# Expert-choice routing on 32 partitions with a threshold, modulation sums of 512 columns, and a final norm by token block

## The chip, the cores and the metric

The kernel runs on one core of one Trainium2 chip. The core has five engines that run side by side and wait for each other by semaphores: TensorE (PE in the profile, with PEld for its weight loads), VectorE (DVE), ScalarE (ACT), GpSimd (POOL) and SyncE (SP), and 16 DMA engines that move data between the chip's memory and its on-chip buffers. The metric is the device time of one execution in microseconds, the median of the runs shown. Lower is better.

## The reference

Two transformer blocks follow one another on a sequence of 512 tokens of width 1024. The first holds an mLSTM layer and a short-convolution layer, each with an MLP of width 4096. The second has a modulation vector for each of two conditions, attention (windowed and latent) over the tokens and 256 context tokens, and a mixture of 16 experts in which each expert chooses its 64 tokens. A final RMS norm ends it. Everything is float32. What the change touches is this:

```python
mod   = silu(c) @ w_mod + b_mod             # (1024) @ (1024, 6144), six vectors of 1024
mod_c = silu(c_ctx) @ w_mod + b_mod         # of which the kernel needs the first two
...
x = x + g_a * mix                           # attention's output, 512 x 1024
h2 = modulate(rmsnorm(x, norm_ffn), sh_f, sc_f)
aff = softmax(h2 @ w_router)                # 512 x 16
vals, idx = top_k(aff.T, 64)                # 64 tokens for each expert
xs = h2[idx]                                # gathered rows, 16 x 64 x 1024
y = (silu(xs @ w_gate) * (xs @ w_up)) @ w_down * vals
x = x + g_f * zeros.at[idx].add(y)
return rmsnorm(x, norm_final)
```

## The kernel before

The residual lies in on-chip memory with the 1024 features on 128 partitions, in 8 pieces of 512 tokens (`self.x`). The large products are made of three TensorE instructions on a high and a low part of each float32 operand (`mm3`, L90 to L94). Each piece of weights comes by a transfer on SyncE's queue; ScalarE casts its high part (L85) and VectorE subtracts the low part (L86), and TensorE takes both.

The program is written engine by engine through a tile framework. A planner at compile time puts the instructions of each engine in order with costs of its own: an instruction that is ready in its plan can be drawn ahead of one that is not, and `keep_in_program_order` ties single instructions. On the chip each engine then runs its instructions in that fixed order, and so does each engine's queue of transfers. A buffer of a pool is one of a ring (its `tag` and `bufs`); a tile that takes a used buffer waits for the last reader.

`mods` (L829) is a generator that is stepped between the pieces of the two MLPs of the first block. It computes the modulation products on VectorE: for each of 24 column groups of 256 and each half of the 1024 rows it loads a tile of 128 x 4 x 256 (L872, four buffers of tag `b4`) and multiplies and adds its four 256-column slices into a running sum (L877, L881), for two condition vectors in the first 8 groups and one in the others. `rows` adds the 128 partitions with matmuls against ones, and `columns` transposes the result into `self.mod`.

`attention_out` (L1382) makes the attention's output product in 8 pieces. After each, VectorE adds it into the residual (L1427), ScalarE squares the new piece and VectorE or GpSimd adds the squares (`Sumsq.add`, L194 and L196), and TensorE adds this piece's part of the router's logits (`stats`, L1402). The column sums of the squares (L207, four matmuls that run as eight instructions) give the tokens' norms (L156 to L162) and with them the logits (L1433).

`route` (L1437) has the softmax over 16 experts on tokens by partition, four transposes to experts by partition (L1452, 16 x 512) and a copy (L1454). Meanwhile TensorE transposes the residual to tokens by partition, ScalarE scales it (L1473), and ScalarE's queue stores it in four pieces to memory (`h2d`, L1474). These four use the buffers `ha` and `wh`; `wh` is a ring of three. The load of the final norm's weights (L1675) takes the next buffer of that ring and stands in the same queue. VectorE finds the 64 largest of each expert in eight rounds: the eight largest (L1478), then these replaced by -1 (L1480). The marked entries are transposed back (L1485), compared (L1487), counted by matmuls with a triangle of ones (L1489, L1491) to the rank of each chosen token (L1494), and turned into one-hot matrices (L1507). A matmul with these gives the token numbers and weights of each pair of experts (`slots`, L1517 to L1523), and GpSimd gathers the rows from the stored copy (`fetch`, L1529). Pairs 0 and 1 are fetched in `route`, the others in the expert loop.

`moe` (L1562) runs over 8 pairs of experts. The weights come in pieces of 1 MB through a ring of buffers (L1550); 15 are started before `route`. The last pair's output goes in four quarters of 256 columns directly to tokens by partition: product (L1595), weighting (L1707), high and low part (L1709, L1710), two matmuls for each of four token blocks (L1718, L1719), squares with their sums (L1721). Then one sum, root and reciprocal (L1726 to L1728) serve all four blocks, ScalarE and VectorE scale the halves (L1731, L1732), and two queues store the output (L1733).

## Time and profile before

| | |
|---|---|
| median of 3 runs | 1812.56 us (1810.69 to 1812.74) |
| profiled execution, its own time | 1812.28 us |
| its span, first to last instruction | 1810.4 us |
| mean granted clock of TensorE, share of full | 0.984 |
| busy: VectorE, ScalarE, GpSimd | 56%, 38%, 4% |
| moved | 254.47 MB, 141 GB/s over the span |

Times in the profile are microseconds from the span's start. A row of a group gives the line, engine and operation, what is written and read (buffer numbers left out), its shape and count, the busy time and the mean of one instruction in ns, and after the bar the idle time of the engine before it and what ended most of it. The first block lies up to about 1200 us, attention from there to 1475, its output product to 1525, the routing to 1555, and the experts from there to the end.

### The profile page before, as it was taken

What the parts mean: (1) busy time and instruction counts of PE and PEld (TensorE: products, weight loads), DVE (VectorE), ACT (ScalarE), POOL (GpSimd) and SP (SyncE); (2) the same over time, 40 slices, a digit from 0 to 9 for tenths busy, and PEclk for the clock granted to TensorE, in tenths of its full rate; (3) what the DMA queues carried; (4) which work ended last, traced back from release to release, by engine and by line L of the source; (5) the groups of instructions that cost most, each with busy time, mean ns of one, the idle gap of its engine ahead of it and who ended that gap; (6) DMA issues with size and microseconds to landing.
All of it is one profiled execution on the core that took longest, in us unless ns stands there. A gap on an engine that the chain in (4) does not pass through costs nothing.

```text
span 1810.4 us, 24232 instructions
## 1 busy us (share of the span) xinstructions
PE 1747.0 (96%) x9763; PEld 1375.6 (76%) x9763; DVE 1009.1 (56%) x1930; ACT 680.7 (38%) x1228; POOL 80.5 (4%) x100
## 2 busy tenths in 40 slices
PE   7999999999999999999999999989899999799997
PEld 5798898777787888898787878888788887334444
DVE  4554575366756774536455554678776743433332
ACT  4344345333322442244323333344666642111112
POOL 1000000000000000000000001013000001000000
PEclk9899999999999999999999999989999999899999
DMA  6221432244544222322444333220100047799993
GB/s 196 71 70 48 147 110 93 94 140 140 163 140 140 94 93 94 116 93 94 139 140 139 120 105 105 70 75 12 25 13 9 20 142 302 272 419 420 420 417 123
DMA packets 157447, 254.47 MB, mean 141 GB/s; under 512 B 20223, under 2 KB 124056, under 8 KB 145432
## 3 DMA queue, kind: packets, MB, share of 16 engines
q1 hardware_dynamic: 152304, 244.70, 38.7%
q10 hardware_dynamic: 3528, 3.98, 0.7%
q0 software_dynamic: 1504, 4.26, 0.6%
q8 instruction: 76, 1.25, 0.3%
q14 instruction: 35, 0.29, 0.0%
HBM read 248.72 MB, written 4.20 MB: 140 GB/s over the span
## 4 chain that ended last, share of the span: by engine, by line
PE 90%; DVE 5%; ACT 3%; issue 1%; DMA 1%; SPq 0%; DVEq 0%; POOL 0%; ACTq 0%
PE ps L92 22%; PE ps L94 22%; PE ps L93 22%; PE ps L1626 7%; PE ps L1605 3%; PE ps L1185 2%; PE ps L1170 2%; PE pw L1323 1%; PE ps L1588 1%; PE pw L1322 1%; PE ps L1587 1%; ACT wh L85 1%; PE ps L1573 1%; DVE th L301 1%; PE ps L1595 0%
## 5 line engine op out<-in xcount | busy, mean ns | idle before, releaser
L92 PE MATMUL ps<-op,wh 128*128 128x512 f32 (+1 forms) x1808 | 653.3, 367 | 7.0 <-ACT wh L85 2.2
L94 PE MATMUL ps<-op,wl 128*128 128x512 f32 (+1 forms) x1808 | 657.9, 366 | 2.2 <-DVE wl L86 2.2
L93 PE MATMUL ps<-op,wh 128*128 128x512 f32 (+1 forms) x1808 | 658.0, 366 | 0.9 <-DVE op L105 0.7
L86 DVE TENSOR_TENSOR wl<-raw,wh 128x1024 fp32r<-128x1024 f32 x210 | 258.1, 1233 | 256.1 <-ACT wh L85 255.5
L92 PEld LDWEIGHTS ps<-op,wh 128*128 128x128 f32 x1808 | 338.1, 189 | 70.5 <-issue 3.3
L93 PEld LDWEIGHTS ps<-op,wh 128*128 128x128 f32 x1808 | 341.8, 189 | 61.3 <-DVE op L105 1.3
L94 PEld LDWEIGHTS ps<-op,wl 128*128 128x128 f32 x1808 | 341.7, 189 | 60.5 <-DVE wl L86 2.9
L85 ACT CAST wh<-raw 128x1024 fp32r<-128x1024 f32 x210 | 219.9, 1052 | 385.6 <-PE ps L93 350.1
L688 DVE TENSOR_TENSOR t<-t,ps 128x512 f32<-128x512 f32 x96 | 65.8, 686 | 112.0 <-PE ps L94 111.8
L1626 PE MATMUL ps<-mw,xs 128*64 128x512 f32 x400 | 115.3, 600 | 0.0
L881 DVE SCALAR_TENSOR_TENSOR u<-b,csilu,u 128x256 f32<-128x256 f32 x224 | 103.9, 492 | 7.7 <-DMA b<-in_w_mod_dram 3.9
L637 ACT ACTIVATE t<-ps 128x512 f32<-128x512 f32 x64 | 38.0, 594 | 109.0 <-PE ps L94 108.9
L92 PE MATMUL ps<-wh,op 128*128 128x256 f32 x256 | 75.3, 295 | 0.1
L1626 PEld LDWEIGHTS ps<-mw,xs 128*64 128x64 f32 x400 | 33.4, 138 | 52.9 <-issue 50.5
L93 PE MATMUL ps<-wl,op 128*128 128x256 f32 x256 | 72.4, 284 | 0.0
L94 PE MATMUL ps<-wh,op 128*128 128x256 f32 x256 | 71.7, 285 | 0.0
L1140 DVE TENSOR_REDUCE sm<-pw 128x1 f32<-128x768 f32 (+2 forms) x64 | 54.1, 854 | 27.4 <-PE pw L1323 14.2
L196 POOL TENSOR_TENSOR acc<-acc,t 128x512 f32<-128x512 f32 x21 | 28.1, 1337 | 605.4 <-ACT t L194 604.8
L92 PEld LDWEIGHTS ps<-wh,op 128*128 128x128 f32 x256 | 49.1, 192 | 4.2 <-ACT og L532 2.3
L93 PEld LDWEIGHTS ps<-wl,op 128*128 128x128 f32 x256 | 49.0, 192 | 0.2
L1580 DVE TENSOR_SCALAR xs<-ps,Ap 128x128 f32<-128x128 f32 x32 | 13.0, 408 | 64.5 <-PE ps L1573 57.3
L94 PEld LDWEIGHTS ps<-wh,op 128*128 128x128 f32 x256 | 48.3, 191 | 0.1
(467 smaller groups left out, 2158.7 us busy)
## 6 DMA issues: line engine op xcount, KB each, us to landing
raw<-in_w_mlp_up_dram SPq DMA_DIRECT2D x32, 1024.0 KB, 5.5
raw<-in_w_mlp_down_dram SPq DMA_DIRECT2D x32, 1024.0 KB, 5.0
mw<-in_w_gate_dram SPq DMA_DIRECT2D x26, 1024.0 KB, 16.6
b<-in_w_mod_dram SPq DMA_DIRECT2D x48, 512.0 KB, 4.7
mw<-in_w_up_dram SPq DMA_DIRECT2D x24, 1024.0 KB, 18.0
mw<-in_w_down_dram SPq DMA_DIRECT2D x19, 1024.0 KB, 19.9
raw<-in_w_in_conv_dram SPq DMA_DIRECT2D x12, 1024.0 KB, 5.1
raw<-in_w_in_mlstm_dram SPq DMA_DIRECT2D x11, 1024.0 KB, 5.4
```

The lines of the kernel that those rows point to most:

```text
L85: nc.scalar.copy(h, raw[:, k0:k0 + kk])
L86: (eng or nc.vector).tensor_sub(lo, raw[:, k0:k0 + kk], h.bitcast(F32))
L92: mm(out, st[0], mv[0], start=first, stop=False)
L93: mm(out, st[0], mv[1], start=False, stop=False)
L94: mm(out, st[1], mv[0], start=False, stop=last)
L637: nc.scalar.activation(t, src, AF.Relu)
L688: nc.vector.tensor_add(y[i], y[i], p)
L881: nc.vector.scalar_tensor_tensor(acc[v], raw[:, k], c, acc[v], op0=OP.mult, op1=OP.add)
L1140: nc.vector.reduce_max(nm[e], p[e][:, 256:256 + n], axis=AX.X, negate=self.sink is None)
L1170: nc.tensor.transpose(pt[:, x * 128:(x + 1) * 128], self.P[e][:, m * 128:(m + 1) * 128], net.ident)
L1605: nc.tensor.matmul(py[dh][e * 64:e * 64 + 64], aT[:, fh * 2 + f, e * 64:e * 64 + 64], r[e][:, f, dh * 512:dh * 512 + 512], start=fh + f == ...
L1626: nc.tensor.matmul(p[e * 64:e * 64 + 64], xs[:, k, e * 64:e * 64 + 64], r[e][:, k % 4], start=k == 0, stop=k == 7, tile_position=(0, e * 64))
```

## The change

It has three parts. In `mods` two neighbouring groups of 256 columns are taken together: a load is 128 x 2 x 512, so that four loads cover the rows, and each instruction on VectorE covers 512 columns; the vector of 32 ones is a broadcast of an existing one. In `attention_out` and `route` the last square is not added on VectorE but summed by matmuls of its own into the same columns. The affinities are laid out as 32 partitions of 256 (partition `16 h + e` holds expert `e` for the token blocks `2 t + h`), so that each expert has two lists. Eight rounds give the 64 largest of each list in falling order; the last round replaces nothing. The second list is moved to the first's partitions by a matmul with 16 columns of the identity, the larger of each list's entry and the other list's entry in reverse order is taken, and the smallest of these 64 is the expert's threshold. A transposition hands it to all partitions. A token is chosen if its affinity is above the threshold, or equal to it and among the first so many; the ranks are counted for both kinds. The one-hots of the first two experts are made before the second two. In `moe` the four matmuls of the high part come before the four of the low part, and sum, root and reciprocal are made for each token block by itself.

```diff
--- before.py
+++ after.py
@@ -832,8 +832,7 @@
         cs = self.cs
         self.mod = self.c([128, 48, 2], name="modc")
         nc.vector.memset(self.mod, 0.0)
-        ones = self.c([128, 32], name="ones32")
-        nc.gpsimd.memset(ones, 1.0)
+        ones = self.ones.to_broadcast([128, 32])
 
         def rows(acc):
 
@@ -858,36 +857,31 @@
                 nc.vector.tensor_copy(self.mod[:, 2 * j - 6:2 * j + 2, 0].rearrange("p (i f) -> p f i", f=2), col)
 
         sums, t = [], None
-        for j in range(24):
+        for j in range(1, 24, 2):
             nv = 2 if j < 8 else 1
-            if len(sums) % 2 == 0:
-                pair = self.t([128, 2, 256], tag="u")
-            if nv == 2:
-                acc = [pair[:, 0], pair[:, 1]]
-            else:
-                acc = [pair[:, len(sums) % 2]]
-            sums += acc
-            for hf in range(2):
-                raw = self.t([128, 4, 256], tag="b4")
-                nc.sync.dma_start(raw, a["w_mod_2"][0][hf * 512:(hf + 1) * 512, j * 256:(j + 1) * 256].rearrange("(k p) n -> p k n", p=128))
+            acc = [self.t([128, 2, 256], tag="u") for _ in range(nv)]
+            sums += [acc[v][:, h] for h in range(2) for v in range(nv)]
+            for k2 in range(KD // 2):
+                raw = self.t([128, 2, 512], tag="b4")
+                nc.sync.dma_start(raw, a["w_mod_2"][0][k2 * 256:(k2 + 1) * 256, (j - 1) * 256:(j + 1) * 256].rearrange("(k p) n -> p k n", p=128))
                 for v in range(nv):
-                    for k in range(4):
-                        c = cs[:, v, hf * 4 + k:hf * 4 + k + 1]
-                        if hf + k == 0:
-                            o = nc.vector.tensor_scalar(acc[v], raw[:, k], c, None, op0=OP.mult)
-                            if v == 0 and j % 2 == 0:
-                                self.tc.keep_in_program_order(o)
+                    o = acc[v].rearrange("p h n -> p (h n)")
+                    for k in range(2):
+                        c = cs[:, v, k2 * 2 + k:k2 * 2 + k + 1]
+                        if k2 + k == 0:
+                            i = nc.vector.tensor_scalar(o, raw[:, k], c, None, op0=OP.mult)
+                            if v == 0:
+                                self.tc.keep_in_program_order(i)
                         else:
-                            nc.vector.scalar_tensor_tensor(acc[v], raw[:, k], c, acc[v], op0=OP.mult, op1=OP.add)
-            if j % 2:
-                yield
-                if len(sums) == 4:
-                    t = rows(sums)
-                    sums = []
-                yield
-                if t is not None:
-                    columns(t, j, nv)
-                    t = None
+                            nc.vector.scalar_tensor_tensor(o, raw[:, k], c, o, op0=OP.mult, op1=OP.add)
+            yield
+            if len(sums) == 4:
+                t = rows(sums)
+                sums = []
+            yield
+            if t is not None:
+                columns(t, j, nv)
+                t = None
         nc.vector.tensor_add(self.mod, self.mod, self.vc[:, 128:176][:, :, None].to_broadcast([128, 48, 2]))
         self.A = self.c([128, 8, 3], name="modA")
         na, nf = self.vc[:, 88:96], self.vc[:, 96:104]
@@ -1425,9 +1419,17 @@
             if k:
                 stats(k - 1)
             nc.vector.scalar_tensor_tensor(self.x[:, k], p, self.mod[:, 16 + k, 0:1], self.x[:, k], op0=OP.mult, op1=OP.add)
-            ss.add(self.x[:, k])
+            if k < KD - 1:
+                ss.add(self.x[:, k])
+        sq = self.t([128, S])
+        nc.scalar.activation(sq, self.x[:, KD - 1], AF.Square)
         stats(KD - 1)
-        cols, _ = self.colsum(ss.acc)
+        pc = self.p()
+        for n, src in enumerate((ss.acc, sq)):
+            for c in range(4):
+                nc.tensor.matmul(pc[:, c:c + 1], src[:, c * 128:(c + 1) * 128], self.ones, start=n + c == 0, stop=n == 1,
+                                 skip_group_check=True)
+        cols = self.rstd_cols(pc[:, 0:4], 4, 1.0 / D)
         lg = self.sm([128, 64])
         for c in range(4):
             nc.vector.scalar_tensor_tensor(lg[:, c * 16:c * 16 + 16], pl[:, c * 16:c * 16 + 16], cols[:, c:c + 1], shw,
@@ -1447,11 +1449,12 @@
         ri = self.sm([128, 4])
         nc.vector.reciprocal(ri, sm)
         nc.vector.tensor_tensor(lg, lg, ri[:, :, None].to_broadcast([128, 4, 16]), op=OP.mult)
+
         pT = self.p()
-        for c in range(4):
-            nc.tensor.transpose(pT[0:16, c * 128:(c + 1) * 128], lg[:, c], self.ident)
-        aT = self.t([16, S], tag="aT")
-        nc.vector.tensor_copy(aT, pT[0:16])
+        for i in range(2):
+            nc.tensor.transpose(pT[0:32, i * 128:(i + 1) * 128], lg[:, 2 * i:2 * i + 2].rearrange("p c e -> p (c e)"), self.ident)
+        aT = self.t([32, 256], tag="aT")
+        nc.vector.tensor_copy(aT, pT[0:32, 0:256])
         tri = self.t([128, 2, 128], BF, tag="tri")
         nc.gpsimd.memset(tri[:, 1], 1.0)
         nc.vector.tensor_scalar(tri[:, 0], self.tok[:, 0:128], self.tok[:, S:S + 1], None, op0=OP.is_ge)
@@ -1472,42 +1475,58 @@
                     nc.tensor.transpose(p[:, j * 128:(j + 1) * 128], self.x[:, hf * 4 + j, c * 128:(c + 1) * 128], self.ident)
                 nc.scalar.activation(t[:, hf * 512:hf * 512 + 512], p, AF.Copy, scale=cols[:, c:c + 1])
             nc.scalar.dma_start(hd[c], t)
-        wk = aT
+
+        wk, top = aT, self.sm([32, 64])
         for r in range(8):
-            v = self.sm([16, 8])
+            v = top[:, 8 * r:8 * r + 8]
             nc.vector.max(v, wk)
-            nw = self.t([16, S], tag="aT")
-            nc.vector.match_replace(out=nw, in_to_replace=v, in_values=wk, imm_value=-1.0)
-            wk = nw
+            if r < 7:
+                nw = self.t([32, 256], tag="aT")
+                nc.vector.match_replace(out=nw, in_to_replace=v, in_values=wk, imm_value=-1.0)
+                wk = nw
 
         pT = self.p()
-        for c in range(4):
-            nc.tensor.transpose(pT[:, c * 16:c * 16 + 16], wk[:, c * 128:(c + 1) * 128], self.ident[0:16, 0:16])
-        sel = self.t([128, 4, 16], BF, tag="sel")
-        nc.vector.tensor_scalar(sel, pT[:, 0:64].rearrange("p (c e) -> p c e", c=4), 0.0, None, op0=OP.is_lt)
-        pp = self.p()[:, 0:64].rearrange("p (c e) -> p c e", c=4)
+        nc.tensor.matmul(pT[0:16, 0:64], self.ident[0:32, 16:32], top, start=True, stop=True)
+        m, th = top[0:16], self.sm([16, 1])
+        nc.vector.tensor_tensor(m, m, pT[0:16, 0:64][:, ::-1], op=OP.max)
+        nc.vector.tensor_reduce(th, m, axis=AX.X, op=OP.min)
+        pT = self.p()
+        nc.tensor.transpose(pT[:, 0:16], th.to_broadcast([16, 128]), self.ident[0:16, 0:16])
+
+        sel = self.t([128, 4, 2, 16], BF, tag="sel")
+        T = pT[:, 0:16][:, None, :].to_broadcast([128, 4, 16])
+        nc.vector.tensor_tensor(sel[:, :, 0], lg, T, op=OP.is_gt)
+        nc.vector.tensor_tensor(sel[:, :, 1], lg, T, op=OP.is_equal)
+        pp = self.p()[:, 0:128].rearrange("p (c s e) -> p c s e", c=4, s=2)
         nc.tensor.matmul(pp, tri[:, 0], sel, start=True, stop=False, skip_group_check=True)
         for c in range(3):
-            nc.tensor.matmul(pp[:, c + 1:], tri[:, 1], sel[:, c:c + 1].to_broadcast([128, 3 - c, 16]), start=False, stop=c == 2,
+            nc.tensor.matmul(pp[:, c + 1:], tri[:, 1], sel[:, c:c + 1].to_broadcast([128, 3 - c, 2, 16]), start=False, stop=False,
                              skip_group_check=True)
+        for c in range(4):
+            nc.tensor.matmul(pp[:, :, 1], tri[:, 1], sel[:, c:c + 1, 0].to_broadcast([128, 4, 16]), start=False, stop=c == 3,
+                             skip_group_check=True)
+        both = self.t([128, 4, 2, 16])
+        nc.vector.tensor_mul(both, pp, sel)
         rank = self.t([128, 4, 16], tag="rank")
-        nc.vector.tensor_mul(rank, pp, sel)
+        nc.vector.tensor_add(rank, both[:, :, 0], both[:, :, 1])
         self.rank = rank
         self.oh, self.slot, self.g = {}, {}, {}
         self.slots_all = self.c([128, 8, 8], name="slots")
-        self.onehots(0)
         for pr in range(2):
+            self.onehots(0, pr)
             self.slots(pr)
             self.fetch(pr)
 
-    def onehots(self, q):
-
-        self.oh[q] = [self.t([128, 256], F32R, tag="oh") for _ in range(4)]
+    def onehots(self, q, half=None):
+
+        if not half:
+            self.oh[q] = [self.t([128, 256], F32R, tag="oh") for _ in range(4)]
+        e0, n = (0, 4) if half is None else (2 * half, 2)
         for c in range(4):
             self.nc.vector.tensor_tensor(
-                self.oh[q][c].rearrange("p (e s) -> p e s", s=64),
-                self.tok[:, 1:65][:, None, :].to_broadcast([128, 4, 64]),
-                self.rank[:, c, 4 * q:4 * q + 4][:, :, None].to_broadcast([128, 4, 64]), op=OP.is_equal)
+                self.oh[q][c][:, e0 * 64:e0 * 64 + n * 64].rearrange("p (e s) -> p e s", s=64),
+                self.tok[:, 1:65][:, None, :].to_broadcast([128, n, 64]),
+                self.rank[:, c, 4 * q + e0:4 * q + e0 + n][:, :, None].to_broadcast([128, n, 64]), op=OP.is_equal)
 
     def slots(self, pr):
 
@@ -1713,23 +1732,25 @@
                 for c in range(2, 4):
                     tokens(X[4 + c], 1, c)
             sl = slice((j % 2) * 256, (j % 2) * 256 + 256)
+            for i, part in enumerate((h, lo)):
+                for c in range(4):
+                    nc.tensor.matmul(X[j // 2 * 4 + c][:, sl], oT[:, c * 128:(c + 1) * 128], part, start=False, stop=i == 1,
+                                     skip_group_check=True)
             for c in range(4):
                 Xc = X[j // 2 * 4 + c][:, sl]
-                nc.tensor.matmul(Xc, oT[:, c * 128:(c + 1) * 128], h, start=False, stop=False, skip_group_check=True)
-                nc.tensor.matmul(Xc, oT[:, c * 128:(c + 1) * 128], lo, start=False, stop=True, skip_group_check=True)
                 sq = self.t([128, 256])
                 nc.scalar.activation(sq, Xc, AF.Square, accum_out=ssq[:, c * 4 + j:c * 4 + j + 1])
             if j == 1:
                 for c in range(4):
                     nc.vector.tensor_mul(res[c][:, 0:512], X[c], nf[:, 0:512])
-        ss, cols = self.sm([128, 4]), self.sm([128, 4])
-        nc.vector.reduce_sum(ss, ssq.rearrange("p (c j) -> p c j", j=4), axis=AX.X)
-        nc.scalar.activation(cols, ss, AF.Sqrt, scale=1.0 / D, bias=self.eps)
-        nc.vector.reciprocal(cols, cols)
         o = out[0].rearrange("(c p) d -> c p d", p=128)
         for c in range(4):
-            nc.scalar.activation(res[c][:, 0:512], res[c][:, 0:512], AF.Copy, scale=cols[:, c:c + 1])
-            nc.vector.scalar_tensor_tensor(res[c][:, 512:1024], X[4 + c], cols[:, c:c + 1], nf[:, 512:1024], op0=OP.mult, op1=OP.mult)
+            ss, col = self.sm([128, 1]), self.sm([128, 1])
+            nc.vector.reduce_sum(ss, ssq[:, c * 4:c * 4 + 4], axis=AX.X)
+            nc.scalar.activation(col, ss, AF.Sqrt, scale=1.0 / D, bias=self.eps)
+            nc.vector.reciprocal(col, col)
+            nc.scalar.activation(res[c][:, 0:512], res[c][:, 0:512], AF.Copy, scale=col)
+            nc.vector.scalar_tensor_tensor(res[c][:, 512:1024], X[4 + c], col, nf[:, 512:1024], op0=OP.mult, op1=OP.mult)
             (nc.sync, nc.scalar)[c % 2].dma_start(o[c], res[c])
 
     def block2(self, cols, out):
```

## Rows read from the trace of the kernel before

**Rows 1.** The page, part 1: busy us, share of the span, instructions.
```profile
PE 1747.0 (96%) x9763; PEld 1375.6 (76%) x9763; DVE 1009.1 (56%) x1930; ACT 680.7 (38%) x1228; POOL 80.5 (4%) x100
```

**Rows 2.** Waits of TensorE over the span: us in total, times, longest.
```profile
PE ps L1485 <- DVE aT L1480: 7.3, 1, 7.3
PE ps L1573 <- DMA wl<-h2d,slots: 4.8, 1, 4.8
...
PE ps L94 <- DVE wl L86: 2.2, 3, 1.4
```

**Rows 3.** Chain that ended last, 1525 to 1557: start us, us, what.
```profile
1527.03 0.70 DVE acc L196
...
1527.87 1.04 PE ps L207 x8
...
1532.49 1.04 PE ps L1452 x4
1533.56 0.69 DVE aT L1454
...
1545.43 0.75 DVE aT L1480 x2
...
1546.93 0.23 DVE sel L1487
...
1547.82 0.43 DVE oh L1507
...
1548.39 1.64 PE ps L1517 x7
...
1550.50 4.35 DMA wl<-h2d,slots
```

**Rows 4.** Groups of VectorE instructions by line, 1530 to 1552 us.
```profile
L1478 DVE MAX8 sm<-aT 16x8 f32<-16x512 f32 x8 | 5.5, 682 | 0.3
...
L1507 DVE TENSOR_TENSOR oh<-tok,rank 128x256 fp32r<-128x256 f32 x6 | 2.2, 416 | 0.0
```

**Rows 5.** Timeline, 1518 to 1560 us, TensorE: start us, us, engine, line, what.
```profile
1525.33 2.07 PE L1402 MATMUL ps<-wr,xres 128*128 128x16 f32 x16
```

**Rows 6.** The same timeline, ScalarE's queue of transfers and GpSimd.
```profile
1536.17 0.34 ACTq L1474 DMA_DIRECT2D h2d<-ha  x1
...
1541.67 0.34 ACTq L1675 DMA_DIRECT2D wh<-in_norm_final_dram  x1
...
1542.10 0.39 ACTq L1474 DMA_DIRECT2D h2d<-wh  x1
...
1551.88 1.10 POOL L1529 DMA_INDIRECT wl<-h2d,slots  x1 [0.31 <-issue]
```

**Rows 7.** DMA view, 1541 to 1549 us: busy tenths, slices of 0.2 us.
```profile
DMA  9997541046999798998989998631100000000000
```

**Rows 8.** DMA view, 1530 to 1537.5 us: queue, packets, MB, share.
```profile
q1 hardware_dynamic: 376, 2.82, 96.8%
```

**Rows 9.** Timeline, 1778 to 1811 us, TensorE in the first quarter of the output.
```profile
1787.03 0.38 PE L1718 MATMUL ps<-ys,aT 128*128 128x256 f32 x1
...
1787.36 0.39 PE L1719 MATMUL ps<-ys,aT 128*128 128x256 f32 x1
```

**Rows 10.** Chain that ended last, 1795 to 1811 us.
```profile
1799.55 0.48 PE ps L1719 x4
...
1800.13 1.20 ACT t L1721 x6
...
1801.36 0.18 DVE sm L1726
...
1803.52 1.32 DVE wl L1732 x2
```

**Rows 11.** The page, part 5: the modulation sums with an addition.
```profile
L881 DVE SCALAR_TENSOR_TENSOR u<-b,csilu,u 128x256 f32<-128x256 f32 x224 | 103.9, 492 | 7.7 <-DMA b<-in_w_mod_dram 3.9
```

**Rows 12.** Timeline of VectorE, 229.9 to 236.5 us: the modulation sums.
```profile
230.32 6.35 DVE L881 SCALAR_TENSOR_TENSOR u<-b,csilu,u 128x256 f32<-128x256 f32 x7
```

## The prediction

> **What bounds the kernel now.** I read the page's first part, then the waits of TensorE, then the chain of work that ended last in two stretches (1525 to 1557 and 1795 to 1811 us), then the timeline and the DMA view of those stretches. TensorE is busy 96% of the span [rows 1], so nothing that runs beside its matmuls pays unless it ends one of its waits. Its largest waits are 7.3 us for the last round of the token choice and 4.8 us for the gather; in the whole first block three waits for a low half of weights make 2.2 us [rows 2]. The route stage is the one place where work off TensorE sets the end. There VectorE forms a single chain: copy, eight rounds, small steps, one-hots, slots, and then the gather, which starts at 1550.50 and takes 4.35 us [rows 3]. TensorE starts the experts as soon as it lands. The list of its waits holds no transfer of expert weights, and their buffers come free with TensorE's own progress, so what the gather gains is passed on to the end in full.
>
> **The choice of tokens.** From the end of the copy (1534.25) to the end of the last replacement (1546.18) eight rounds take 11.93 us, 1.49 each [rows 3]. Width costs VectorE about 1.0 ns a column: 256 columns took 416 ns in L1507, 64 took 230 in L1487 [rows 3, 4]. At 256 columns in place of 512 each of the two long instructions of a round (the maximum took 682 ns at 512, [rows 4]) loses 0.26 us, and a round costs 0.97. Eight of them without the last replacement (0.49) make 7.27: a gain of 4.66. The bounds are 0.75 (width costs nothing, only the last replacement goes) and 6.4 (half the time, and the last replacement gone); the slope is from the same engine, so I keep the value within 0.5. Two transposes replace four that took 1.04 [rows 3]: gain 0.4 of at most 0.52. The copy loses 256 columns: 0.26.
>
> What the change adds stands on the same chain. Before, 1546.18 to 1547.82 is 1.64: to TensorE and back (0.75), one compare (0.23), four matmuls and a product (0.66) [rows 3]. After: to TensorE and back with one matmul (0.75), maximum and minimum (0.5), back again with the threshold (0.65), two compares (0.5), eight matmuls (0.7), a product of 128 columns and a sum (0.54): 3.64, so 2.0 lost. No row shows a matmul that moves 16 partitions or a reversed read; I price them as the nearest hop and the nearest small instruction, and bound the loss by 1.2 and 3.0. The one-hots of two experts come first, so the first slots wait for four half-width instructions and 4 matmuls, not for four whole ones and 7 matmuls: 1547.82 to 1550.03 was 2.2 [rows 3], I take 1.45, a gain of 0.75 (0.3 to 1.0).
>
> The square that is no longer added on VectorE removes 0.70 [rows 3]. But the column sums are now 16 matmuls where they were 8 (1.04, [rows 3]), and TensorE has 16 router matmuls just before them, 2.07 from 1525.33 [rows 5]. The old sums ended at 1528.91, 3.58 after 1525.33. Thirty-two such matmuls at the pace of those sixteen take 4.14, and 3.6 if the pause between the two eights, in which TensorE waits for the last residual, is filled. TensorE's own queue takes the place of the addition: 0, bounds 0.5 gained and 0.55 lost.
>
> Chain of the choice: 4.66 + 0.4 + 0.26 - 2.0 + 0.75 = 4.1. The gather could start at 1546.4.
>
> **What is late next.** The gather reads what the ScalarE queue stores. The fourth store is issued at 1542.10, behind the load of the final norm's weights at 1541.67 [rows 6], which takes the buffer of the second store and so waits until that has landed. The change leaves these instructions and the ring of three buffers as they are. The 16 DMA engines are busy with the load and this store until 1546.8 (the 29th slice of 0.2 us) [rows 7]; I add 0.3 until the store counts as landed, an estimate, so 1547.1. The second gather followed its engine's last work by 0.31 [rows 6], so the gather starts near 1547.4 or 1547.5. From 1530 to 1537.5 only the weight queue moved packets (376), although the first store was issued at 1536.17 [rows 6, 8]: the stores come behind the last weight prefetch, which the column sums release and which doesn't move. So the 0.4 of the shorter transposes doesn't reach the store. Of the 4.1 us 3.0 are kept, and TensorE's wait for the rounds becomes one for the store.
>
> The Trainium skill, DMA: Bandwidth & Descriptors, section Queues, rings and completion order, says that each engine alternates between the queues that have work, packet by packet; by that rule the stores would share the engines from their issue, their landing would follow the transposes, and 3.4 us would be kept.
>
> **The modulation sums.** 256 vector instructions of 256 columns become 128 of 512; the 48 loads of 512 KB stay, each with longer rows. The 224 with an addition took 492 ns each, 104 us busy [rows 11], so a wide one takes between 492 and 984 ns: never more in all than now. All of it lies beside the first block's matmuls and is hidden there except at one place. At 230.32 seven of these instructions took 6.35 us [rows 12], with additions on GpSimd beside them, and a low half of weights stood behind them on VectorE; that is the longest of TensorE's three waits, 1.4 us [rows 2]. The wide form can end that wait or lengthen it by one more instruction or two. Bounds: 1.4 gained, 2 lost; I take 0. If the cover goes, what is queued behind a sum that waits for its load is the weights' low halves, and TensorE waits for those. The memset of 32 ones on GpSimd goes, and nothing waits for it: 0.
>
> **The final norm.** With all high-half products ahead of the low-half ones, TensorE no longer stands for the low half after its first product. In the first quarter that is 0.33 between 1787.03 and 1787.36 [rows 9], where a stream issues one each 0.12 [rows 10]: 0.2. Two quarters have it, and the third's low halves may move behind the last expert product, 0.5 at most; in the fourth the sums end on ScalarE's squares, which start no earlier. I take 0.35, bounds 0 and 0.9. Then one reduction, root and reciprocal for four token blocks become four of each, and the first block need not wait for the last square. Before, the reduction starts at 1801.36, and the last products run from 1803.52 [rows 10]; the output's transfers follow one another at the DMA engines' full rate from there, so what counts is when the first block is ready. It gains 0.25 if ScalarE does all four squares (0.4 each, [rows 10]) before the first root, and 1.0 if the first root comes after the second square; ScalarE then has three more roots ahead of its copies, at most 0.9. Value 0.45, bounds 0.3 lost and 1.1 gained.
>
> **Sum.** 3.0 + 0 + 0.35 + 0.45 = 3.8. The profiled execution took 1812.28 us (its span 1810.4 and 1.9 around it), so 1808.5 for it; the median of the runs shown is 0.28 above it, so 1808.8. The least change that can be told here is 0.2%, 3.6 us: below 1808.9 is faster, above 1816.2 slower. The forecast lies on that edge.
>
> **Rivals.** (a) The store does not gate. If the fourth store comes ahead of the norm's load, it has landed before the slots are ready and the choice itself sets the gather: 4.1 to 4.6 in place of 3.0, and 1807.4. For it: the load was drawn forward from the end of the kernel to this place, so a planner chose it, with a close margin; against: nothing in the change moves what that choice is made from. (b) The added hops cost their upper bound and TensorE's queue loses 0.3: the choice then gains 2.8, and with nothing at the tail the time is 1810. For it: every hop is a start from an idle TensorE; against: so were the old ones, from which the price is taken. (c) Slower: each of the 12 pairs of wide sums holds a weights' low half behind it on VectorE for as long as the sums at 230.32 do. At 1.4 us a pair eleven more cost 15.4, and the time is 1824; from three on it eats the gain, from six on it shows as slower. For it: a wide instruction can't be interrupted for a low half that becomes ready. Against: 256 narrow ones are caught once now, and a wide one that is held up by a GpSimd addition does twice the work in the same hold. (d) The one wait of 1.4 goes as well: 1807.4.
>
> The Trainium skill, SBUF — State Buffer, section SBUF: two separate sides, calls the port pair of VectorE and GpSimd an exclusive lock held for a whole instruction; the slow stretch agrees [rows 12], and fewer, wider instructions would meet the lock less often, which speaks against (c).
>
> **Chances.** Forecast 62% (of it 56 in 100 below the edge), (a) 16%, (b) 11%, (c) 4%, (d) 7%. Faster: 0.35 + 0.14 + 0.06 = 0.55; slower 0.04; same 0.41. The range for eight in ten goes from (a) with the tail's better bound, 1805.5, to (b) with a lost microsecond and a half in the sums, 1811.5.
>
> **What would show it.** After the change the rounds are 0.97 apart and seven of them replace; the gather starts near 1547.5 with its slots ready a microsecond earlier; the fourth store is still behind the norm's load; the column sums end 3.6 us or more after the first router matmul of the last eight; the wide sums take 0.6 to 0.75 us. The forecast is wrong if the gather follows its slots at once, if VectorE's way from the copy to the first slots is longer than 13.5 us, or if the waits for low halves in the first block exceed 4 us.

## The result, and the profile after the change

The changed kernel takes 1803.37 us (median of 5, 1802.44 to 1803.72) against 1812.56 us of the kernel before (1810.69 to 1813.97): a ratio of 0.9949, 95% interval 0.9938 to 0.9960, so 9.2 us less where 3.8 were forecast. Its span is 1801.6 us where it was 1810.4. Below, instants of the two traces are compared at the same TensorE instruction.

The page's first part and its row of the sums, where [rows 1, 11] stood:

```profile
PE 1741.1 (97%) x9772; PEld 1372.8 (76%) x9772; DVE 979.1 (54%) x1813; ACT 680.7 (38%) x1231; POOL 80.0 (4%) x99
L876 DVE SCALAR_TENSOR_TENSOR u<-b,csilu,u 128x512 f32<-128x512 f32 x112 | 79.7, 748 | 5.7 <-DMA b<-in_w_mod_dram 4.6
```

TensorE is not only idle less, it is busy 5.9 us less although it has nine instructions more. So part of the gain is matmuls that ran faster, by their own pace or by a higher clock, and the forecast did not look for either. One wide sum took 748 ns, in the range of the forecast.

TensorE's waits after (engine, tile, line, releaser: us in total, times, longest), beside [rows 2]:

```profile
PE ps L1592 <- DMA wl<-h2d,slots: 6.8, 1, 6.8
PE ps L1489 <- DVE sm L1482: 2.8, 1, 2.8
PE ps L94 <- DVE wl L86: 0.9, 2, 0.4
```

The wait for the rounds fell from 7.3 to 2.8, the one for the gather rose from 4.8 to 6.8, and the single wait of 1.4 for a low half is gone. The chain of waits names the gather's releaser (start, us, what; it begins with the first transpose of the affinities):

```profile
1526.38 0.61 PE ps L1455 x2
...
1531.13 4.56 DMA h2d<-wh
1535.69 0.02 issue
1535.72 0.34 ACTq L1694
...
1536.15 5.27 DMA h2d<-wh
...
1542.28 4.60 DMA wl<-h2d,slots
1546.88 0.14 issue
1547.01 1.94 PE ps L1592 x8
```

The second store lands, which lets the norm's load go (L1694), and behind that in the same queue the fourth store; the gather follows it. This is the gate that the forecast named. The first gather starts 15.90 us after the first transpose of the affinities (1526.38), where it took 18.01.

Where the 8.8 us of span arise is read from the lead: how much earlier the same TensorE instruction starts in the changed kernel's trace. 0.35 is lost at the start; 3.2 gained between 73 and 84 us, 0.7 in small steps to 236, 1.65 at 237, 0.7 in small steps to 624; 2.15 lost from there to 637; 0.85 gained to 1486, 1.55 from there to 1491; 0.55 lost before the last eight router matmuls, ahead of which the changed kernel now has eight of the column sums; 2.4 gained from these to the first expert matmuls and 0.8 after them, nearly all at the tail. The forecast had looked at the 1.65, the route and the tail alone. The largest is this one, seen in windows of the two kernels (start:end, length, busy us and count of PE, PEld, DVE, ACT, POOL, then the granted clock, DMA share, GB/s), of the kernel before and then of the changed one:

```profile
73.00:84.00 11.00, 11.00 (x39) 7.41 (x37) 4.30 (x8) 1.67 (x5) 0.00 (x0) 0.53 0.31 95
```

```profile
73.00:84.00 11.00, 11.00 (x63) 8.76 (x63) 4.65 (x8) 2.50 (x6) 0.00 (x0) 0.84 0.32 95
```

The same program text runs here, after the same idle time of 1.9 us. Before, TensorE's clock was at the lower level (1.2 GHz, 0.5 of full) for 10.2 us; after, for 3.4. In the same time it issued 39 and 63 matmuls.

### The profile page after: what moved, and what is told of

It is laid out like the page before. It is cut to its first block, busy times and chain, and to the rows that moved or that the text cites. A ratio compares the mean times of both kernels' runs of the same rounds, so it can differ in the third digit from the quotient of the medians.

```text
span 1801.6 us, 24154 instructions
## 1 busy us (share of the span) xinstructions
PE 1741.1 (97%) x9772; PEld 1372.8 (76%) x9772; DVE 979.1 (54%) x1813; ACT 680.7 (38%) x1231; POOL 80.0 (4%) x99
## 4 chain that ended last, share of the span: by engine, by line
PE 90%; DVE 4%; ACT 3%; DMA 1%; issue 1%; SPq 0%; ACTq 0%; POOL 0%; POOLq 0%; DVEq 0%
PE ps L92 22%; PE ps L93 22%; PE ps L94 22%; PE ps L1645 7%; PE ps L1624 3%; PE ps L1179 2%; PE ps L1164 2%; PE pw L1317 1%; PE ps L1607 1%; PE pw L1316 1%; PE ps L1606 1%; ACT wh L85 1%; PE ps L1592 1%; DMA h2d<-wh 1%; DVE th L301 1%
## 5 line engine op out<-in xcount | busy, mean ns | idle before, releaser
L876 DVE SCALAR_TENSOR_TENSOR u<-b,csilu,u 128x512 f32<-128x512 f32 x112 | 79.7, 748 | 5.7 <-DMA b<-in_w_mod_dram 4.6
L92 PEld LDWEIGHTS ps<-wh,op 128*128 128x128 f32 x256 | 48.3, 189 | 4.2 <-ACT og L532 2.3
L641 DVE CAST op<-t 128x512 fp32r<-128x512 f32 x64 | 27.1, 424 | 38.9 <-ACT t L639 25.3
```

The costliest lines, as they stand in the source:

```text
L92: mm(out, st[0], mv[0], start=first, stop=False)
L876: nc.vector.scalar_tensor_tensor(o, raw[:, k], c, o, op0=OP.mult, op1=OP.add)
```

## Experiments

Two theories stood at the start. L: the low clock falls differently from run to run and is no part of the change, the sums won about 2.5 and the route 2.4. M: the new sums themselves brought all 5.4 us of the lead at 257. A later pair was A (what counts is the 32 ones, whose 128 bytes moved the buffers behind them) against W (what counts is the width of the sums). S, D, I and T are named in the expectations that test them. Where the expectations say 3.35 for the lead gained near 73, the two traces show 3.2. All medians are against the kernel before in the same runs (1812.45 to 1812.98).

**The sums alone** (both hunks in `mods`).

> The kernel before with the modulation sums alone in the new form (512 columns, loads of 128 x 2 x 512, ones by broadcast). Theory L (low clock by chance): of the 5.4 us that the changed kernel had gained by 257 us the sums made about 2.5 (the wait of 1.4 for a low half near 236 is gone, and some 1.0 in small waits between 84 and 272); the other 3.35 came from a shorter stretch at the lower of TensorE's two clocks near 73 us (3.4 us in place of 10.2), which does not belong to the change. So the time is about 1810.0, the waits for low halves are 1.0 us or less in all, and the low stretch near 73 has any of the lengths 3.4, 6.8 or 10.2. Rival M (the sums did it all): the order that the wide sums bring shortens the low stretch itself; the time is 1807.1 and the stretch near 73 is 3.4 us long again. My forecast's own term was 0: 1812.5.

Measured: 1807.38 (0.9972, 0.9962 to 0.9982), 5.1 less: nearer to M. But its trace had 6.8 us of low clock near 73, and single runs went from 1805.44 at a mean clock of 0.986 to 1809.01 at 0.983. So M's mechanism fell (the stretch was not short again), while L's price of the sums was too small by half. The waits for low halves are 0.8 in all.

**The choice of tokens and column sums alone** (the hunks in `attention_out` and `route`).

> The kernel before with the new column sums and the new choice of tokens alone. Both theories: the gather starts 15.9 us after the first transpose of the affinities in place of 18.0, behind the fourth store, and the time is 2.1 to 2.4 less, about 1810.2. Theory L: the low stretches are those of neither trace but any. Rival M: the low stretch near 73 is 10.2 us long as in the kernel before, since nothing of the first block is changed. My forecast had 3.0 here (1809.5).

Measured: 1809.17 (0.9983, 0.9974 to 0.9992), 3.3 less; the low clock near 73 lasted 6.8 us with nothing changed there, where M had 10.2. In the trace the gather starts 15.61 us after the first transpose (1530.36 to 1545.97), so 2.4 earlier than before, as both theories had it. The rest of the 3.3 may be the clock's: its runs had a mean granted clock of 0.985, those of the kernel before 0.984.

**Both kernels once more**, with no edit.

> The kernel before itself once more. Theory L: the stretches at the lower clock lie elsewhere or have other lengths than in the first trace (10.2 us near 73 and 3.4 near 1486 in that one), the span moves by 1.7 us for each 3.4 us of them in which TensorE is busy, and single times spread over 3 us. Rival M: the same stretches to the slice, near 73 again 10.2 us long, and spans within 1 us of 1810.4.

> The changed kernel itself once more. Theory L: other stretches at the lower clock than in its first trace (3.4 us near 73 and 6.8 near 625), with the span moved accordingly by 1.7 to 3.4 us, and times that spread up to 1807. Rival M: the same stretches, and spans within 1 us of 1801.6.

Measured: 1812.91 (1.0006, 0.9997 to 1.0015) and 1803.91 (0.9958, 0.9945 to 0.9972). Theory L missed for the kernel before: its stretches near 73 and 1486 came back. It held for the changed kernel, whose second trace has the long stretch near 73:

```profile
73.00:84.00 11.00, 10.53 (x38) 7.36 (x38) 4.40 (x8) 1.77 (x5) 0.00 (x0) 0.53 0.32 95
```

and still a span of 1802.1, since its stretch near 626 was 3.4 us long and not 6.8. So the 3.2 near 73 is chance, and 2.15 of it was given back near 626. What stayed was a lead that grew by about 0.1 every ten or twenty microseconds wherever matmuls of 256 columns ran: their starts were 119.2 ns apart on average in the three traces with the old sums (the two of the kernel before, and the choice alone) and 117.9 in the three with the new ones (some 1950 of them between 84 and 1180 us).

**The 32 ones alone.** In the compiled program the tiles `op`, which hold the high and low parts of the activations, begin at byte 40512 of each partition before and at 40384 after, because `ones32` is no longer taken. The buffers `t`, `u` and `b4`, which also lie behind the ones, move down by the same 128 bytes; the weights' tiles `wh` and `wl` stay.

```diff
-        ones = self.c([128, 32], name="ones32")
-        nc.gpsimd.memset(ones, 1.0)
+        ones = self.ones.to_broadcast([128, 32])
```

> The kernel before with one edit: the 32 ones are a broadcast of an existing one, so that 128 bytes a partition are no longer taken and the operand tiles behind them (op, t, u, b4) lie 128 bytes lower. Same instructions in the same order. Theory A (addresses): the 256-column matmuls of the first block follow one another every 117.9 ns in place of 119.2, as in every kernel with the new sums; some 1950 of them make 2.5 us, so 1810.0, with the wait of 1.4 near 236 still there. Rival W (the wide sums on VectorE make TensorE's pace): 119.2 as before, and 1812.5. My forecast counted this edit as nothing.

And the changed kernel with these two old lines back:

> The changed kernel with the 32 ones taken and set again as before, so that the operand tiles lie where they lay before. Theory A (addresses): the spacing of the 256-column matmuls is 119.2 ns again, and the time 1803.6 + 2.5 = 1806.1. Rival W: 117.9, and 1803.6.

Measured: 1810.63 (0.9989, 0.9980 to 0.9998) and 1808.06 (0.9975, 0.9966 to 0.9984). The second is 4.2 more than the changed kernel's 1803.91, and the spacing explains 2.5 of it. The trace of the second also has 3.4 us of low clock near 1484, which neither trace of the changed kernel has there; it cost 1.55 between the first two traces. Spacings are 117.9 and 119.2, as A says. A run of 120 such matmuls without a pause shows it. A row names the moving operand first, here `op`, and the stationary one second, here a piece of weights. The timeline's first and last of them (start, us, engine, line), in the kernel before, with the 32 ones alone changed, and in the changed kernel with them back; the last fence is the window over the 120 in the kernel before:

```profile
788.37 0.28 PE L92 MATMUL ps<-op,wh 128*128 128x256 f32 x1
...
802.65 0.28 PE L94 MATMUL ps<-op,wl 128*128 128x256 f32 x1
```

```profile
783.74 0.28 PE L92 MATMUL ps<-op,wh 128*128 128x256 f32 x1
...
797.82 0.27 PE L94 MATMUL ps<-op,wl 128*128 128x256 f32 x1
```

```profile
787.11 0.28 PE L92 MATMUL ps<-op,wh 128*128 128x256 f32 x1
...
801.39 0.28 PE L94 MATMUL ps<-op,wl 128*128 128x256 f32 x1
```

```profile
788.36:802.66 14.30, 14.30 (x121) 14.29 (x120) 4.53 (x6) 6.49 (x15) 3.64 (x3) 1.00 0.25 74
```

First to last 14.28, 14.08 and 14.28 us at the full clock; TensorE and its weight loads are busy for all of it. The weights lie where they lay, so the pace hangs on where `op` and the buffers behind it lie. Whether it is the reading of the moving operand or the loads that are slowed is not shown. W is out for the pace. The single runs with the ones alone also show the clock's chance at its widest: 1804.54 at a mean clock of 0.988, 1814.71 at 0.981, with one program. The Trainium skill, TensorE: Matmul & The Clock Gate, Part 1: The HAM clock gate, says that the gate's watch runs on by itself and is not reset when a kernel starts. These runs do not contradict it (the changed kernel's stretch near 73 was 3.4 us long in one trace and 10.2 in the other), but none tests it.

**The wide sums alone**, with the 32 ones left in place.

> The kernel before with the wide sums, but the 32 ones taken and set as before, so that the operand tiles stay where they were. Theory A (addresses and one wait): the 256-column spacing stays 119.2 ns, the wait for the low half near 236 is gone, and the time is 1812.5 - 1.6 = 1810.9. Rival W (the wide sums bring more than that wait): the time is nearer to the 1807.4 of the sums with the ones changed.

Measured: 1810.58 (0.9994, 0.9984 to 1.0005), 2.1 less by the medians, not told from nothing by the interval. Its single runs fall apart by the clock: five took 1814.4 to 1815.0 at a mean clock of 0.981, six 1809.4 to 1811.1 at 0.983 to 0.985. The trace is clearer: spacing 119.2, and of the wait for a low half, 1.5 us in the kernel with only the ones changed (first fence), 0.4 is left at most with only the sums widened (second):

```profile
PE ps L94 <- DVE wl L86: 2.4, 3, 1.5
```

```profile
PE ps L94 <- DVE wl L86: 0.9, 2, 0.4
```

So theory A and the one wait account for most of the sums' part: 1.9 and 2.1 by the medians, 4.0 of 5.1. That wait hangs on timing too: in the kernel before with seven matmuls more near 71 (below) its longest was 0.4 with the old sums.

**Two other places for the operand tiles**: 64 bytes taken and not used in the changed kernel, and 192 with the store freed (below).

```diff
         ones = self.ones.to_broadcast([128, 32])
+        self.c([128, 16], name="pad")      # or [128, 48]
```

> The changed kernel with 64 bytes a partition taken and not used where the 32 ones lay, so that the operand tiles begin 64 bytes higher than in the changed kernel and 64 lower than in the one before. Theory A (addresses): the spacing of the 256-column matmuls takes another value than 117.9 ns: 119.2 or between (up to 1806.1), or less (1801). Rival W: 117.9, and 1803.6.

> As the last kernel with 192 bytes in place of 64: the operand tiles begin 64 bytes above their place in the kernel before. Theory A: a fourth pair of spacings. If only the place within 256 bytes counts, both lie between those seen (116.8 to 119.9 where the operands stand in the array, 117.0 to 118.2 where they move), and the time between 1799.5 and 1803.2. Rival: the spacings are those of the kernel before (119.9 and 118.2), since what counts is an order of buffers and not a place; 1803.2.

Measured: 1802.77 (0.9951, 0.9938 to 0.9965) and 1805.25 (0.9955, 0.9941 to 0.9968). The expectations of these runs, and the one with the store freed and 64 bytes, name the two roles the wrong way round: up to 235 us `op` is the stationary operand (rows `ps<-wh,op`), later it moves (`ps<-op,wh`). With `op` moving the spacing is 116.8 ns at byte 40448 (64 bytes), against 119.9 at 40512 and 118.3 at 40384; with `op` stationary it is 118.2, 118.2 and 117.0. The 120 matmuls took 13.88:

```profile
784.00 0.28 PE L92 MATMUL ps<-op,wh 128*128 128x256 f32 x1
...
797.88 0.28 PE L94 MATMUL ps<-op,wl 128*128 128x256 f32 x1
```

At 40576 (192 bytes) it is 117.4 to 119.3 from place to place with `op` moving and 119.8 with `op` stationary, and the time is 2 us above the range expected; the matmuls of 512 columns were 234.3 ns apart where every other trace has 233.3, which over some 3300 of them is 3.3 us. The effect is real, its rule is open.

**The store freed**: the norm's load stays in its written place on ScalarE's queue.

```diff
-                nc.scalar.dma_start(nf, a["norm_final_2"]...)
+                self.tc.keep_in_program_order(nc.scalar.dma_start(nf, a["norm_final_2"]...))
```

> The changed kernel, with the load of the final norm's weights held in its written place on ScalarE's queue (the seventh pair of experts) and not drawn ahead of the fourth store; nothing else moves. Theory S (that store behind the load sets the gather): the store is issued near 1533.7 and lands by 1538, the gather starts when its slots are ready, near 1539.7 in place of 1542.3, and the time is 1803.6 - 2.6 = 1801.0. Rival D (the DMA engines, full until 1537, set the store's landing): the store lands at 1540.5 or later, and the time is 1802.7 or more.

Measured: 1800.39 (0.9930, 0.9917 to 0.9944), so theory S holds. The timeline has the fourth store, the first gather and the experts' first transposes:

```profile
1534.49 0.33 ACTq L1477 DMA_DIRECT2D h2d<-wh  x1
...
1539.86 1.07 POOL L1548 DMA_INDIRECT wl<-h2d,slots  x1 [12.18 <-DVE oh L1526]
...
1544.41 1.94 PE L1592 MATMUL ps<-ident,wl 128*128 128x128 f32 x8 [3.60 <-DMA wl<-h2d,slots]
```

The gather now follows its slots, 12.88 us after the first transpose (1526.98). So the choice of tokens itself gains 5.1, and the changed kernel left 3.0 of it behind the store.

With the 64 bytes besides:

> The changed kernel with both earlier edits: the norm's load in its written place, and 64 bytes a partition taken and not used ahead of the operand tiles. Theory A (addresses): 256-column matmuls at 118.2 ns where the weights stand in the array (some 740, 84 to 235 us) and 116.8 where the operands do (some 1200), so 0.9 us less than with the first edit alone: 1799.5. Rival (the two gains do not add, as the sum of many small paces hides in other waits): 1800.4.

Measured: 1799.68 (0.9921, 0.9908 to 0.9935), as expected of A, but 0.7 is within the spread.

**The clock.** Seven matmuls without use in the idle time near 71, in the changed kernel with the store freed and in the kernel before; and sixteen in the wait for the gather.

```diff
         pc = self.p()
+        for _ in range(7):
+            self.tc.keep_in_program_order(nc.tensor.matmul(pc, self.identb, self.cmask, start=True, stop=True))
...
                 p = self.p()
+                for _ in range(0 if pr or hf else 16):
+                    self.tc.keep_in_program_order(nc.tensor.matmul(p[:, 0:256], self.identb, self.tri, start=True, stop=True))
```

> The changed kernel with the norm's load in its written place, and seven matmuls of 512 bf16 columns, whose result is overwritten, in TensorE's idle time of 1.9 us near 71 us, ahead of the transposes there. Theory I (the idle time is what lowers the clock): no stretch at the lower clock near 73, 1.7 to 5.1 us saved against a run that has one of 3.4 or 10.2: about 1797.5. Rival T (the thin matmuls after it lower the clock, 32 rows or 128 columns each): a stretch of 3.4 us or more near 75 in spite of them, and 1800.4.

> The kernel before with the seven matmuls in the idle time near 71 us. Theory I (the low clock near 73 is a cost of its own, 1.7 to 5.1 us, that has nothing to do with the change): no low stretch near 73, a spread of single times under 5 us, and a median of 1810.0. Rival T (another low stretch takes its place later): 1812.5, the sum of low stretches as before.

> The changed kernel with the norm's load in its written place, and sixteen matmuls of 256 bf16 columns, whose result is overwritten, in TensorE's wait for the first gather. Theory I (idle time lowers the clock): the stretch at the lower clock that now lasts over the gather's landing ends before it, the first 3 us of expert products run at the full clock, and 1.5 us are saved: 1798.9. Rival T: the stretch lasts as long as now, or the extra matmuls end after the gather has landed: 1800.4 to 1801.5.

Measured: 1799.28 (0.9919, 0.9905 to 0.9932), 1809.70 (0.9986, 0.9978 to 0.9995) and 1799.92 (0.9928, 0.9914 to 0.9941). In the first there is no low clock near 73, but one of 3.4 us at 1479, and the time is 1.1 less than with the store freed alone, where theory I had 2.9. In the second there is 3.4 us near 75 all the same, and the time is 3.0 less; the wait for a low half that fell to 0.4 is about 1 of that. So neither theory holds alone. The idle time is a part of the cause: every trace without the seven matmuls has 3.4 to 10.2 us near 73. That the thin matmuls behind it are another is likely and not shown, since no run changes them. In the third the expert products start at the full clock; the windows 1546 to 1548 without the sixteen, and with them:

```profile
1546.00:1548.00 2.00, 2.00 (x8) 0.65 (x8) 1.14 (x3) 1.47 (x4) 0.00 (x0) 0.57 0.03 8
```

```profile
1546.00:1548.00 2.00, 2.00 (x10) 0.73 (x12) 1.18 (x3) 1.95 (x5) 0.00 (x0) 1.00 0.00 0
```

The sixteen end 0.4 before the gather lands. By the medians it is 0.5 us, not told from nothing.

**The final norm alone** (the hunk in `moe`).

> The kernel before with the new final norm alone. My forecast's term: 0.8 less, 1811.7, of it 0.35 before the last expert product of the last quarter and 0.45 after it. Rival (the three more roots on ScalarE eat it): 1812.5, and the time from the last expert product to the end as before.

Measured: 1811.64 (0.9993, 0.9984 to 1.0002), 1.0 less by the medians, as forecast and unclear by itself.

**All that gained, together.**

> The changed kernel with all that gained: the norm's load in its written place, 64 bytes a partition taken and not used ahead of the operand tiles, the seven matmuls near 71 us and the sixteen in the wait for the gather. If the gains add: 1799.7 (with the first two edits) less 1 to 3 for the stretch near 73 and less 1.0 for the one after the gather, about 1797. Rival (low clock moves elsewhere, as with the fill near 71 alone, where one of 3.4 us came at 1479): 1799.5.

Measured: 1797.03 (0.9912, 0.9899 to 0.9925), 15.6 less than the kernel before and 6.3 less than the changed one's first median. The sum came out as expected, though several of its terms are within the spread by themselves.

## Why the prediction was wrong

The route held in kind, the modulation sums failed. The route's 3.3 by the medians is near the forecast's 3.0 in part by luck: in the traces the gather came only 2.1 (the changed kernel) to 2.4 (the route alone) earlier.

By the parts run alone, the medians give 1.9 for the 32 ones, 2.1 for the wide sums, 3.3 for choice and column sums and 1.0 for the tail: 8.2 of the 8.5 to 9.2. The second and the fourth are not told from nothing by their intervals.

- **The failed step is the modulation sums at 0.** "The memset of 32 ones on GpSimd goes, and nothing waits for it: 0": nothing did wait for it, but its 128 bytes went too, and 1.3 ns less in some 1950 matmuls is 2.5 us. No wait shows this; TensorE's busy time does. The sums as a whole made 5.1 by the medians.
- **The one wait of 1.4** was put between 1.4 gained and 2 lost, and taken as 0. It went: its end was the better bound, and rival (d) came true beside the forecast. Rival (c) did not: 12 pairs of wide sums leave 0.9 of waits for low halves where 2.2 were. The rule of the Trainium skill cited against (c) (SBUF — State Buffer, section SBUF: two separate sides) was not tested by this: in the changed kernel GpSimd's additions (4.03 us from 226.63) met no wide sum.
- **The gate** was right in place and kind. Its price was 0.9 off: 15.90 from the first transpose to the gather where the forecast's 1547.45 makes 14.96. The last packet of the store ran 14.70 after the transposes (1541.08), where the forecast had 14.31, and the gather came 1.2 after that packet, not 0.6. The landing followed the packet by 0.34, near the 0.3 that was estimated; the rest lies between the landing and the gather on GpSimd. The forecast read [rows 8] as stores that wait behind the last weight prefetch. That reading is wrong: in the kernel before the first store's packets began at 1537.89, ahead of the last weight packet at 1538.73, and in the changed kernel both queues moved packets from 1531.6 to 1532.8 (below: queue, packets, MB, share; q10 has the stores, q1 the weights). The changed kernel's first store had its first packet at 1531.56, 2.1 after its issue at 1529.45, and until then the weight queue alone moved. The norm's load, issued at 1535.72 with no weights moving, took 1.2 to its first packet, so some 0.9 of the 2.1 is left that the other queue may account for. The rule on alternating queues (the Trainium skill, DMA: Bandwidth & Descriptors, section Queues, rings and completion order) is neither shown nor refuted by these rows.

```profile
q10 hardware_dynamic: 78, 0.32, 64.6%
q1 hardware_dynamic: 31, 0.14, 30.1%
```

- **The choice** was priced at 4.1 and made 5.1 once freed. The rounds are 0.96 apart (0.97 forecast). From the end of the last maximum to the end of the rank it took 2.73, where 3.64 was counted and the way before had 1.64: the added hops cost 1.1, under their lower bound of 1.2. This error did not reach the time, since the store set the gather. The rows, from the copy on:

```profile
1527.03 0.41 DVE L1457 COPY aT<-ps 32x256 f32<-32x256 f32 x1 [0.70 <-PE ps L1455]
...
1534.18 0.42 DVE L1482 MAX8 sm<-aT 32x8 f32<-32x256 f32 x1
1534.74 0.27 PE L1489 MATMUL ps<-sm,ident 32*16 32x64 f32 x2 [2.82 <-DVE sm L1482]
...
1535.64 0.20 PE L1494 MATMUL ps<-ident,sm 16*128 16x16 f32 x1 [0.63 <-DVE sm L1492]
...
1537.10 0.23 DVE L1511 TENSOR_TENSOR rank<-t 128x64 f32<-128x64 f32 x1
```

- **The column sums** were right: 7.30 us from the first of the router matmuls to the transposes, 7.16 before; 0.14 lost where 0 was forecast.
- **The tail** was forecast at 0.8. The trace of the changed kernel shows it: the lead grows from 8.1 at 1716 to 8.8 at the end, 0.33 of that after the start of the last high-half products (1790.35, 11.25 before the end; before, 1798.82 and 11.58).
- **The clock** was no term of the forecast, which took the profiled time as fixed; a repetition of the kernel before spread from 1811.32 to 1814.79. The 3.2 near 73 is chance of one pair of traces. The 1.55 at 1486 to 1491 is not: it is in the second pair too (1.57). Both traces of the kernel before have 3.4 us of low clock there. Of the changed kernel's traces, with and without the later edits, seven have none; those with the 32 ones back or with the seven matmuls near 71 have it again. So it goes with the change here; why is open. Over single runs of the same mean granted clock, 0.984, the kernel before averages 1812.4 (23 runs) and the changed one 1804.0 (6 runs): 8.5 of the 9.2 stay.

## What to carry to other kernels

A buffer that is removed moves all that is allocated behind it; where TensorE is busy 96% of the span, compare the distance of starts of one matmul shape before and after, not only its waits. Before a gain of a few microseconds is put down to an edit, compare the granted clock of the same stretch in a second trace of the same program. When a chain on one engine is shortened, look for what stands in the queues of its other inputs, and hold a transfer that is not urgent in its place.

## What the runs showed of the hardware

Matmuls of 256 columns with loads of 128 columns were between 116.8 and 119.9 ns apart at the full clock, by nothing but the place of one operand's tiles and of the buffers behind them, shifted by 64 or 128 bytes. And the clock fell where TensorE had no idle time: in the kernel before, after 24 matmuls of 16 columns and two of 128 at 1482.8 to 1485.6, the clock was at the lower level for 3.4 us from 1486.4 (the window's mean is 0.89, with TensorE busy for all of it); in the changed kernel the same matmuls were followed by none. The four windows are the kernel before, the changed one, and each of them once more.

```profile
1480.00:1495.00 15.00, 15.00 (x77) 12.66 (x76) 4.54 (x7) 3.29 (x4) 1.71 (x2) 0.89 0.65 235
```

```profile
1475.00:1490.00 15.00, 15.00 (x84) 12.81 (x83) 5.09 (x7) 3.34 (x5) 2.82 (x2) 1.00 0.76 268
```

```profile
1480.00:1495.00 15.00, 15.00 (x77) 12.70 (x76) 4.48 (x7) 3.29 (x4) 1.31 (x2) 0.89 0.63 231
```

```profile
1475.00:1490.00 15.00, 15.00 (x84) 12.77 (x84) 5.37 (x7) 3.60 (x5) 2.30 (x2) 1.00 0.74 259
```
